# Top-2 gate and dispatch: the first group loaded in two parts and stored in four, without the small early store

## The chip, the cores and the metric

The kernel runs on one core of one Trainium2 chip. Its compute engines used here are DVE (VectorE) and ACT (ScalarE); SP (SyncE) and ACT issue the DMAs, which run on sixteen DMA engines. The metric is the device time of one execution in microseconds (us), and the time before is the median of three runs.

## The reference

For each of 16 x 1024 tokens there are a row of 512 float32 values and eight router logits. The two largest softmax probabilities are kept, in rising order, and divided by their sum; the row is written twice, once scaled by each.

```python
probs = np.exp(router_logits - logits_max)
probs = probs / np.sum(probs, axis=-1, keepdims=True)
topk_indices = np.argsort(probs, axis=-1)[..., -k:]
topk_probs = np.take_along_axis(probs, topk_indices, axis=-1)
topk_probs = topk_probs / np.sum(topk_probs, axis=-1, keepdims=True)
x_expanded = x[:, :, np.newaxis, :].repeat(k, axis=2)
return (x_expanded * topk_probs[..., np.newaxis]).astype(np.float32)
```

With k = 2 the two weights are sigmoids of the difference between the largest and the second largest logit, with either sign. The input x has 33.5 MB, the output 67.1 MB.

## The kernel before

A "row" in this text is one token on each of 128 partitions: 256 KB to load and 512 KB to store. The 16,384 tokens are 128 such rows, in two groups of 65 and 63 (GROUPS). In a group each partition holds consecutive tokens, so a load or a store of n rows is one contiguous stretch per partition.

Two buffers hold all the data. xs has room for 65 input rows. osp has room for 18 output rows (L), and its first rows also hold the logits and the scratch of the top-2 steps, until the weights WA are there. STORES gives for each store of a group the first row, the number of rows, where the output is built and at which place. Output that is built in "xs" overwrites input rows that have been used already, two places for each output row.

The group's loads are issued first, in the parts that LOADS gives (line 139), all on SP's queue but the first of the second group. After the load that completes the first six rows the two logit loads (lines 144 and 145) are issued, also on SP, and top2_weights computes the weights of both groups: eleven small DVE instructions (lines 26 to 36) and two sigmoids on ACT (lines 37 and 38).

Then each part of the group is multiplied on DVE (line 164) and stored (line 176). The first store of the first group, 3 rows, is issued by ACT; all the others by SP. SP and ACT work through their issues in program order, and an issue waits until the data are ready, with everything behind it on that queue.

A part that is built in osp from place 0 again is cut in two (cuts): the first FREE[g] rows lie where no store is under way, the others wait until the earlier store from the same places has landed. In the second group, ACT makes the last ACT_ROWS rows of the first part with one activation for each row and weight (line 157), and DVE the rest.

The second group's first load, 4 rows, is issued by ACT behind a small activation, the pause (line 128), which waits until the first group's last but one store has landed. The load of 28 rows follows the first group's last store on SP. The load of 31 rows goes into places from which the first group's last store reads, and waits for that store's landing.

Of the kernel before, what the change touches and what calls it, by code (L numbers as in the profile page):

```python
# [1 line left out]

# [4 lines left out]

F32 = mybir.dt.float32
ALU = mybir.AluOpType
ACTF = mybir.ActivationFunctionType  # L10
P = 128


def top2_weights(nc, WA, dlt, room, logits, E):

    tt = nc.vector.tensor_tensor
    hi, lo, n = None, None, E  # L20
    while n > 1:
        n //= 2
        if hi is None:
            a, b = logits[:, :, 0:n], logits[:, :, n : 2 * n]
            nhi, nlo = room(n), b
            tt(nhi, a, b, op=ALU.max)  # L26
            tt(nlo, a, b, op=ALU.min)  # L27
        else:
            a, b = hi[:, :, 0:n], hi[:, :, n : 2 * n]
            nhi, nlo, tmp = room(n), room(n), room(n)  # L30
            tt(tmp, lo[:, :, 0:n], lo[:, :, n : 2 * n], op=ALU.max)  # L31
            tt(nlo, a, b, op=ALU.min)  # L32
            tt(nlo, nlo, tmp, op=ALU.max)  # L33
            tt(nhi, a, b, op=ALU.max)  # L34
        hi, lo = nhi, nlo
    tt(dlt, hi[:, :, 0], lo[:, :, 0], op=ALU.subtract)  # L36
    nc.scalar.activation(WA[:, :, 0], dlt, ACTF.Sigmoid, scale=-1.0)  # L37
    nc.scalar.activation(WA[:, :, 1], dlt, ACTF.Sigmoid, scale=1.0)  # L38

GROUPS = [65, 63]

LOADS = [[6, 28, 31], [4, 28, 31]]
BASE = [0, 1]

STORES = [
    [(0, 3, "osp", 0), (3, 15, "osp", 3), (18, 16, "xs", 0), (34, 15, "osp", 0), (49, 16, "xs", 33)],
    [(0, 16, "osp", 2), (16, 16, "xs", 0), (32, 15, "osp", 0), (47, 16, "xs", 32)],
]  # L50

L = 18

FREE = [3, 2]

ACT_ROWS = 2


@with_exitstack
def kernel(  # L60
    ctx: ExitStack,
    tc: tile.TileContext,
    x: bass.AP,
    router_logits: bass.AP,
    k: bass.AP,
    out: bass.AP,
):
    nc = tc.nc
    B, S, D = x.shape
    E = router_logits.shape[-1]  # L70
    N = B * S
    assert int(k) == 2 and E == 8 and N == P * sum(GROUPS)
    M = N // P

    x_v, o_v, rl_v = [], [], []
    t0 = 0
    for n in GROUPS:
        t1 = t0 + P * n
        x_v.append(
            x.rearrange("b s d -> (b s) d")[t0:t1].rearrange("(p m) d -> p m d", p=P)  # L80
        )
        o_v.append(
            out.rearrange("b s k d -> (b s) k d")[t0:t1].rearrange(
                "(p m) k d -> p m k d", p=P
            )
        )
        rl_v.append(
            router_logits.rearrange("b s e -> (b s) e")[t0:t1].rearrange(
                "(p m) e -> p m e", p=P
            )  # L90
        )
        t0 = t1

    wpool = ctx.enter_context(tc.tile_pool(name="wpool", bufs=1))
    xs = wpool.tile([P, max(GROUPS), D], F32)
    osp = wpool.tile([P, L, 2, D], F32)
    WA = wpool.tile([P, M, 2], F32)
    dlt = wpool.tile([P, M], F32)


    flat = osp.rearrange("p l k d -> p (l k d)")
    taken = [0]

    def room(n):
        o = taken[0]
        taken[0] += M * n
        return flat[:, o : o + M * n].rearrange("p (m n) -> p m n", n=n)

    logits = room(E)

    def place(where, at, n):

        if where == "osp":
            return osp[:, at : at + n]
        return xs[:, at : at + 2 * n, :].rearrange("p (r k) d -> p r k d", k=2)

    m0 = 0
    stores = []
    for g, G in enumerate(GROUPS):
        x0, r = BASE[g], 0  # L120
        for n in LOADS[g]:

            late = g == 1 and r == 0
            if late:


                rows = xs[:, x0 : x0 + 2, :]
                pause = nc.scalar.activation(rows, rows, ACTF.Copy)  # L128
                tc.add_manual_dep(
                    pause.ins,  # L130
                    stores[-2].ins.name,
                    mybir.DependencyInfo(
                        mybir.DependencyClass.Sync, mybir.DependencyReason.DATA
                    ),
                    reason="begin when the store ahead of the last has landed",
                )
                tc.keep_in_program_order(pause)
            queue = nc.scalar if late else nc.sync
            load = queue.dma_start(xs[:, x0 + r : x0 + r + n, :], x_v[g][:, r : r + n, :])  # L139
            tc.keep_in_program_order(load)  # L140
            r += n
            if g == 0 and r == 6:
                n0 = GROUPS[0]
                tc.keep_in_program_order(nc.sync.dma_start(logits[:, :n0], rl_v[0]))  # L144
                tc.keep_in_program_order(nc.sync.dma_start(logits[:, n0:], rl_v[1]))  # L145
                top2_weights(nc, WA, dlt, room, logits, E)
        assert r == G
        for r, n, where, at in STORES[g]:
            og = place(where, at, n)

            again = where == "osp" and at == 0 and r > 0
            cuts = [0, FREE[g], n] if again else [0, n]
            if g == 1 and r == 0:
                cuts = [0, n - ACT_ROWS]
                for j in range(n - ACT_ROWS, n):
                    for k2 in range(2):
                        nc.scalar.activation(  # L157
                            og[:, j, k2, :],
                            xs[:, x0 + r + j, :],
                            ACTF.Copy,  # L160
                            scale=WA[:, m0 + r + j, k2 : k2 + 1],
                        )
            for a, b in zip(cuts, cuts[1:]):
                nc.vector.tensor_tensor(  # L164
                    og[:, a:b],
                    xs[:, x0 + r + a : x0 + r + b, :]
                    .unsqueeze(2)
                    .to_broadcast([P, b - a, 2, D]),
                    WA[:, m0 + r + a : m0 + r + b, :]
                    .unsqueeze(3)  # L170
                    .to_broadcast([P, b - a, 2, D]),
                    op=ALU.mult,
                )

            queue = nc.scalar if g == r == 0 else nc.sync
            stores.append(queue.dma_start(o_v[g][:, r : r + n], og))  # L176
            tc.keep_in_program_order(stores[-1])
        m0 += G


# [1 line left out]
_INS = ['x', 'router_logits', 'k']  # L182
_OUTS = [((16, 1024, 2, 512), 'float32')]

_NUMBERS = {'k': 2}


# [26 lines left out]
```

## Time and profile before

| | us |
|---|---|
| median of three runs (239.55 to 241.16) | 239.67 |
| the profiled execution | 239.64 |
| its span, first to last instruction | 237.9 |
| DVE busy | 139.8 |
| ACT busy | 5.4 |
| HBM read, written | 34.08 MB, 67.11 MB |

The span is what the profile covers of the execution; the remaining 1.7 us lie around it. The page divides the span into 40 slices of about 5.9 us. For each engine a digit gives the busy share of a slice in tenths; for DMA it is the mean busy share of the sixteen engines. Large packets are counted where they end, so neighbouring slices of the DMA line must be read together. A line of the timeline gives start, length, engine, line of code and operation; "SPq" and "ACTq" are issues of DMAs. A line of the DMA view gives what is moved, the issuing queue, the number of issues, their size where it is known and the median time from issue to landing. In a line of the groups the shape is partitions x elements; 1024 elements are one output row, and the last two numbers before the second bar are the busy time in us and the mean of one instruction in ns.

### The profile page before, as it was taken

Reading aid. Unit: us, or ns where it says so; the run is one execution under the profiler, and the core shown is the slowest. Engines: PE = TensorE matmul, PEld = TensorE weight load, DVE = VectorE, ACT = ScalarE, POOL = GpSimd, SP = SyncE. Lnnn points to the kernel's source line nnn. Section 1 sums busy time; section 2 is a strip of 40 time slices with the busy share of each in tenths; the row PEclk is TensorE's granted clock in tenths of the full one; section 3 lists DMA queues with packets and bytes.
Section 4 is the critical chain, followed back from the end, with each engine's and each line's share of the span. In section 5 each row is a group of like instructions: output and inputs, shape, how many; then the busy total and the mean of one; then the engine's idle time right before and its main releaser. Section 6 shows DMA issues by size and latency. Waiting matters only on the chain.

```text
span 237.9 us, 111 instructions
## 1 busy us (share of the span) xinstructions
DVE 139.8 (59%) x22; ACT 5.4 (2%) x8; POOL 0.2 (0%) x4
## 2 busy tenths in 40 slices
DVE  0650499999689999200000009999976999950000
ACT  2000000000000000010000003000000000000000
POOL 0000000000000000000000000000000000000000
DMA  7989998989998989989998999898998989989894
GB/s 266 550 357 481 441 408 375 486 351 496 397 463 353 529 362 465 496 353 415 555 397 350 444 479 470 384 507 364 485 397 386 496 353 507 465 362 518 353 529 176
DMA packets 2448, 101.19 MB, mean 425 GB/s; under 512 B 272, under 2 KB 400, under 8 KB 528
## 3 DMA queue, kind: packets, MB, share of 16 engines
q1 hardware_dynamic: 2160, 98.57, 96.2%
q10 hardware_dynamic: 288, 2.62, 2.6%
HBM read 34.08 MB, written 67.11 MB: 425 GB/s over the span
## 4 chain that ended last, share of the span: by engine, by line
DMA 49%; DVE 39%; SPq 1%; issue 0%; DVEq 0%
DMA xs<-in_x_dram 29%; DVE osp L164 25%; DMA out_dram<-osp 19%; DVE xs L164 14%; SPq L144 0%; SPq L145 0%; SPq L139 0%; SPq L176 0%; DVEq L164 0%
## 5 line engine op out<-in xcount | busy, mean ns | idle before, releaser
L164 DVE TENSOR_TENSOR osp<-xs,WA 128x3072 f32<-128x3072 f32 (+5 forms) x7 | 67.2, 9604 | 63.5 <-DMA xs<-in_x_dram 56.9
L164 DVE TENSOR_TENSOR xs<-xs,WA 128x16384 f32<-128x16384 f32 x4 | 68.9, 17225 | 0.2
L26 DVE TENSOR_TENSOR osp<-osp 128x512 f32<-128x512 f32 x1 | 0.7, 691 | 8.1 <-DMA osp<-in_router_logits_dram 8.1
L157 ACT ACTIVATE osp<-xs,WA 128x512 f32<-128x512 f32 x4 | 2.6, 709 | 37.6 <-DMA xs<-in_x_dram 37.6
L128 ACT ACTIVATE xs<-xs 128x1024 f32<-128x1024 f32 x1 | 1.1, 1056 | 91.1 <-DMA out_dram<-osp 91.1
L37 ACT ACT_TABLE_LOAD x1 | 1.3, 1283 | 0.7 <-PEq L195 0.7
L27 DVE TENSOR_TENSOR osp<-osp 128x512 f32<-128x512 f32 x1 | 0.7, 691 | 0.0
L32 DVE TENSOR_TENSOR osp<-osp 128x256 f32<-128x256 f32 (+1 forms) x2 | 0.7, 352 | 0.0
L34 DVE TENSOR_TENSOR osp<-osp 128x256 f32<-128x256 f32 (+1 forms) x2 | 0.7, 351 | 0.0
L33 DVE TENSOR_TENSOR osp<-osp 128x256 f32<-128x256 f32 (+1 forms) x2 | 0.7, 351 | 0.0
L31 DVE TENSOR_TENSOR osp<-osp 128x256 f32<-128x256 f32 (+1 forms) x2 | 0.7, 350 | 0.0
L37 ACT ACTIVATE WA<-dlt 128x128 f32<-128x128 f32 x1 | 0.3, 315 | 10.0 <-DVE dlt L36 10.0
L36 DVE TENSOR_TENSOR dlt<-osp 128x128 f32<-128x128 f32 x1 | 0.3, 291 | 0.0
L38 ACT ACTIVATE WA<-dlt 128x128 f32<-128x128 f32 x1 | 0.3, 298 | 0.0
L195 POOL MEMSET const-uint8-127<- 128x1 uint8 x1 | 0.1, 102 | 0.0
L195 POOL MEMSET const-bfloat16-1.0<- 128x1 bf16 x1 | 0.1, 101 | 0.0
L195 POOL MEMSET const-float32-0.0<- 128x1 f32 x1 | 0.1, 98 | 0.2 <-issue 0.2
L195 POOL MEMSET const-float32-1.0<- 128x1 f32 x1 | 0.1, 98 | 0.0
## 6 DMA issues: line engine op xcount, KB each, us to landing
out_dram<-osp SPq DMA_DIRECT2D x3, 7680.0 KB, 23.3
xs<-in_x_dram SPq DMA_DIRECT2D x2, 7936.0 KB, 40.7
xs<-in_x_dram SPq DMA_DIRECT2D x2, 7168.0 KB, 35.1
xs<-in_x_dram SPq DMA_DIRECT2D x1, 1536.0 KB, 5.9
out_dram<-osp ACTq DMA_DIRECT2D x1, 1536.0 KB, 24.8
xs<-in_x_dram ACTq DMA_DIRECT2D x1, 1024.0 KB, 24.8
osp<-in_router_logits_dram SPq DMA_DIRECT2D x1, 260.0 KB, 6.2
osp<-in_router_logits_dram SPq DMA_DIRECT2D x1, 252.0 KB, 6.3
```

The source lines that it names most:

```text
L26: tt(nhi, a, b, op=ALU.max)
L27: tt(nlo, a, b, op=ALU.min)
L31: tt(tmp, lo[:, :, 0:n], lo[:, :, n : 2 * n], op=ALU.max)
L32: tt(nlo, a, b, op=ALU.min)
L33: tt(nlo, nlo, tmp, op=ALU.max)
L34: tt(nhi, a, b, op=ALU.max)
L36: tt(dlt, hi[:, :, 0], lo[:, :, 0], op=ALU.subtract)
L37: nc.scalar.activation(WA[:, :, 0], dlt, ACTF.Sigmoid, scale=-1.0)
L128: pause = nc.scalar.activation(rows, rows, ACTF.Copy)
L157: nc.scalar.activation(og[:, j, k2, :], xs[:, x0 + r + j, :], ACTF.Copy, scale=WA[:, m0 + r + j, k2 : k2 + 1],)
L164: nc.vector.tensor_tensor(og[:, a:b], xs[:, x0 + r + a : x0 + r + b, :] .unsqueeze(2) .to_broadcast([P, b - a, 2, D]), WA[:, m0 + r + a : ...
L195: nc = _bacc.Bacc("TRN2", target_bir_lowering=False, num_devices=1)
```

## The change

The first group's loads become two, of 33 and 32 rows, and the logit loads and the top-2 steps follow the first of these. Its stores become four, of 16, 16, 17 and 16 rows. The first is built in osp from place 2 on, like that of the second group; ACT makes its last five rows in ten activations, DVE the other eleven, and SP issues the store, so that all stores are now on SP's queue. The part that uses osp again has two free rows instead of three, and fifteen that wait. The second group's tables are the same.

```diff
-LOADS = [[6, 28, 31], [4, 28, 31]]
+LOADS = [[33, 32], [4, 28, 31]]
...
-    [(0, 3, "osp", 0), (3, 15, "osp", 3), (18, 16, "xs", 0), (34, 15, "osp", 0), (49, 16, "xs", 33)],
+    [(0, 16, "osp", 2), (16, 16, "xs", 0), (32, 17, "osp", 0), (49, 16, "xs", 33)],
     [(0, 16, "osp", 2), (16, 16, "xs", 0), (32, 15, "osp", 0), (47, 16, "xs", 32)],
...
-FREE = [3, 2]
-
-ACT_ROWS = 2
+FREE = [2, 2]
+
+ACT_ROWS = [5, 2]
...
-            if g == 0 and r == 6:
+            if g == 0 and r == LOADS[0][0]:
...
-            if g == 1 and r == 0:
-                cuts = [0, n - ACT_ROWS]
-                for j in range(n - ACT_ROWS, n):
+            if r == 0:
+                cuts = [0, n - ACT_ROWS[g]]
+                for j in range(n - ACT_ROWS[g], n):
...
-            queue = nc.scalar if g == r == 0 else nc.sync
-            stores.append(queue.dma_start(o_v[g][:, r : r + n], og))
+            stores.append(nc.sync.dma_start(o_v[g][:, r : r + n], og))
```

## The prediction, made before the changed kernel ran

> **What bounds the kernel now.** I first read the page's totals, the slices of the span and the DMA queues.
>
> ```profile
> span 237.9 us, 111 instructions
> DVE 139.8 (59%) x22; ACT 5.4 (2%) x8; POOL 0.2 (0%) x4
> DMA  7989998989998989989998999898998989989894
> DMA packets 2448, 101.19 MB, mean 425 GB/s; under 512 B 272, under 2 KB 400, under 8 KB 528
> q1 hardware_dynamic: 2160, 98.57, 96.2%
> q10 hardware_dynamic: 288, 2.62, 2.6%
> DMA 49%; DVE 39%; SPq 1%; issue 0%; DVEq 0%
> ```
>
> The busiest compute engine works 59% of the span. The packets of the two DMA queues take 96.2 + 2.6 = 98.8% of the sixteen engines' span, and only the first and the last slice are thin. So the kernel is bound by DMA throughput without a hole: DVE matters only by when it lets a store be issued. The chain of waits, the last line, names DVE for 39%, but a store that is issued while older packets still run costs nothing; what counts is whether each queue entry is there before the packets ahead of it are gone.
>
> Next come the issues in the timeline (start, length, what), and for each the DMA view of its stretch, whose last figure is the time from issue to landing. First the opening, then the last store of the first group and the second group.
>
> ```profile
> 0.73 0.37 SPq L139 DMA_DIRECT2D xs<-in_x_dram  x1
> 2.10 1.05 SPq L139 DMA_DIRECT2D xs<-in_x_dram  x2
> 15.91 0.38 ACTq L176 DMA_DIRECT2D out_dram<-osp  x1
> 43.00 0.35 SPq L176 DMA_DIRECT2D out_dram<-osp  x1
> 79.13 0.33 SPq L176 DMA_DIRECT2D out_dram<-osp  x1
> 96.39 0.33 SPq L176 DMA_DIRECT2D out_dram<-xs  x1
> 124.71 0.34 SPq L139 DMA_DIRECT2D xs<-in_x_dram  x1
> 157.51 0.34 SPq L176 DMA_DIRECT2D out_dram<-osp  x1
> 211.64 0.33 SPq L176 DMA_DIRECT2D out_dram<-xs  x1
> ```
>
> ```profile
> xs<-in_x_dram SPq DMA_DIRECT2D x1, 1536.0 KB, 5.9
> xs<-in_x_dram SPq DMA_DIRECT2D x1, 7936.0 KB, 45.2
> out_dram<-osp ACTq DMA_DIRECT2D x1, 1536.0 KB, 24.8
> out_dram<-osp SPq DMA_DIRECT2D x1, 7680.0 KB, 23.1
> out_dram<-osp SPq DMA_DIRECT2D x1, 7680.0 KB, 24.4
> out_dram<-xs SPq DMA_DIRECT2D x1, 28.3
> xs<-in_x_dram SPq DMA_DIRECT2D x1, 7936.0 KB, 36.2
> out_dram<-osp SPq DMA_DIRECT2D x1, 22.8
> out_dram<-xs SPq DMA_DIRECT2D x1, 25.4
> ```
>
> Row by row the second fence belongs to the first; of the two loads issued at 2.10 it shows the second (31 rows), which starts at about 2.7. The landings are therefore 6.63, 47.9, 40.7, 66.1, 103.5, 124.7, 160.9, 180.3 and 237.0.
>
> The unit of the sum comes from the end, where nothing but stores runs: 47 rows are stored between the landings at 180.3 and 237.0, so one row of stores takes 56.7 / 47 = 1.207 us; a row of loads has half the bytes, 0.604. It holds elsewhere: the 15 rows after the last load took 66.1 - 47.9 = 18.2 us, 15 x 1.207 = 18.1. The start costs 5.9 - 6 x 0.604 = 2.28 us between the issue of a load on idle engines and its landing, beyond its data.
>
> **The change, part by part.** I rebuild the first group's clock.
>
> ```profile
> 8.05 0.69 DVE L26 TENSOR_TENSOR osp<-osp 128x512 f32<-128x512 f32 x1 [8.05 <-DMA osp<-in_router_logits_dram]
> 12.52 3.36 DVE L164 TENSOR_TENSOR osp<-xs,WA 128x3072 f32<-128x3072 f32 x1 [0.58 <-ACT WA L38]
> 142.25 2.56 ACT L157 ACTIVATE osp<-xs,WA 128x512 f32<-128x512 f32 x4 [37.57 <-DMA xs<-in_x_dram]
> 142.35 15.09 DVE L164 TENSOR_TENSOR osp<-xs,WA 128x14336 f32<-128x14336 f32 x1 [45.98 <-DMA xs<-in_x_dram]
> ```
>
> ```profile
> L164 DVE TENSOR_TENSOR xs<-xs,WA 128x16384 f32<-128x16384 f32 x4 | 68.9, 17225 | 0.2
> L164 DVE TENSOR_TENSOR osp<-xs,WA 128x15360 f32<-128x15360 f32 x1 | 16.2, 16157 | 10.9 <-DMA xs<-in_x_dram 10.9
> L164 DVE TENSOR_TENSOR osp<-xs,WA 128x13312 f32<-128x13312 f32 x1 | 14.0, 14026 | 3.4 <-DMA out_dram<-osp 3.4
> L164 DVE TENSOR_TENSOR osp<-xs,WA 128x12288 f32<-128x12288 f32 x1 | 13.0, 12960 | 2.6 <-DMA out_dram<-osp 2.6
> L164 DVE TENSOR_TENSOR osp<-xs,WA 128x2048 f32<-128x2048 f32 x1 | 2.3, 2285 | 0.0
> L157 ACT ACTIVATE osp<-xs,WA 128x512 f32<-128x512 f32 x4 | 2.6, 709 | 37.6 <-DMA xs<-in_x_dram 37.6
> ```
>
> *Loads in 33 and 32 rows.* The two logit loads stay behind the first load on SP's queue, which is now 27 rows longer: 27 x 0.604 = 16.3 us. So the chain of small DVE steps starts at 8.05 + 16.3 = 24.4 instead of 8.05, and the first multiply at 12.52 + 16.3 = 28.8. DVE idles through those 16.3 us; it is hidden as long as loads fill the engines. SP waits for nothing before the load of 32 rows, so that load follows at once.
>
> *First store.* DVE multiplies 11 rows. Between 12 and 13 rows the step is 14.026 - 12.960 = 1.066 us, so 11 rows take 11.89 and end at 40.7. ACT makes the other five rows in ten activations; four took 2.56 us, so ten take 6.4 and end at 35.2 if they run beside DVE. That they do is shown at 142: 14 rows took 15.09 beside four activations, while 12 and 15 rows without them (12.960, 16.157) give 15.09 by the same step. ACT's first activation waits for the load and the sigmoids; behind it on ACT stands only the pause for the second group, due near 103. The store is issued on SP at 40.74. Its wait holds up the second store on SP, which is not due before 57.9.
>
> *Early store removed.* Its 3 rows leave the stretch of the loads, 3 x 1.207 = 3.6 us of DMA time; the same bytes go out in later stores, so nothing is saved by that. The loads land at 47.9 - 3.6 = 44.3 with every other loss kept. The first store is then issued 44.3 - 40.74 = 3.5 us before they land. Is that enough? In the second group the store issued at 157.51 stood 160.9 - 157.5 = 3.4 us ahead of the last load's landing, and its 16 rows landed 180.3 - 160.9 = 19.4 us later, against 16 x 1.207 = 19.3. So a lead of 3.4 us lost no more than 0.1.
>
> *The reused rows of osp.* The first store lands at 44.3 + 19.3 = 63.6. Meanwhile DVE does 16 rows in place (17.225, to 57.9, second store issued) and the two free rows (2.285, to 60.2; the second of them needs the load that landed at 44.3). The other 15 rows wait for the landing at 63.6 and take 16.157: third store issued at 79.8. The second store lands at 63.6 + 19.3 = 82.9, so the lead is 3.1 us. No row shows exactly this lead. The nearest bounds are 2.28 us, all that a load on idle engines needed including its own start, and 3.4, shown to suffice for a store. I take it as enough, nearer to the 3.4 that concerns a store; at worst 0.3 us is lost.
>
> *After it.* The third store, one of 17 rows, lands at 82.9 + 17 x 1.207 = 103.4, before 103.5; the pause on ACT waits for just that landing. The fourth is issued at 79.8 + 17.2 = 97.0 instead of 96.4, while packets run until 103.4. SP then issues the load of 28 rows behind it, as before, and the last load waits for the fourth store to land, at 124.7 before. From there both kernels are the same, to the end.
>
> *What can be gained.* By units, the loads, the 512 KB of logits (two load rows) and the early store are 65 + 2 + 6 = 73 load rows, 44.1 us; with 0.73 of start and 2.28 of latency the last load would land at 47.1. It lands at 47.9, so 0.8 us is lost somewhere while the early store runs among the loads. If the mix causes all of it, all is gained; if reads alone or the first store on a queue causes it, nothing is. I take half, 0.4, as no row splits it. The pieces per partition stay eight for the first group: three loads and five stores before; after, two loads and four stores, of which the load of 33 rows is built as 2 x 8448 elements and the store of 17 as 2 x 8704.
>
> One rule speaks for a different result. By the rows, stores that follow each other land 19.3 us per 16 rows and 18.1 per 15, in proportion to bytes, so a transfer queued behind another shows no fixed price of its own. The Trainium skill, page DMA: Bandwidth & Descriptors, section Anatomy of one DMA, prices a transfer at about 2 us plus its bytes. Two transfers fewer would then save 4 us and give 235.6, an estimate by that page. Nothing here pays that price except at the start.
>
> **The rivals.** *A. The forecast:* no hole opens, 0 to 0.8 us gained.
>
> *B. A small hole ahead of the first or the third store.* The first is the case in which the change does not do what it says: the last load packets are gone before the store's first packet is there. For it: leads shrink from 47.9 - 43.0 = 4.9 us to 3.5, and to 3.1 at the third store. Against: the 3.4 shown to suffice. It decides when the lead falls under 2.3 to 3.4; each microsecond under costs one. A slip of one or two microseconds gives 239.7 to 241.0.
>
> *C. Slower: DVE and ACT hold each other up while both write the first store.* If ten activations of 709 ns were to run in series with the 11 rows, the issue would come at 40.74 + 7.1 = 47.8. With 2.28 us of lead needed, the hole would be 47.8 - (44.3 - 2.28) = 5.8 us, and the time 245.4. It costs from an issue at 42.0 on. Against it stands the 15.09 beside four activations; for it, only that ten at once are not in the trace.
>
> *D. Faster: a fixed price per transfer.* Fifteen transfers instead of seventeen; if each costs its 2.28 us of latency, 4.6 us go, and the time is 235.0. The landings in proportion to rows speak against it. This is the mechanism of the page's rule above.
>
> **How the numbers follow.** The profiled execution took 239.64 us, 1.74 more than its span of 237.9; the median of three runs is 239.67, with a range up to 241.16, so the profiled one is an ordinary run. A gives 239.64 - 0.4 = 239.2, and 238.8 to 239.7 as its own range. Chances: A 0.76, B 0.14, C 0.07, D 0.03. A difference of about 1%, 2.4 us, is what a measurement here can tell from no change. Only D is faster than that: 0.03. Slower by that much are most of C and a large B: 0.08. The rest, 0.89, is the same. For 8 in 10 the range takes A and the smaller half of B, with 0.2 for scatter below: 238.6 to 240.5.
>
> **What would show it.** In the changed profile: DVE's first small step near 24.4, first multiply near 28.8 and 11.9 us long, the first store issued near 40.7 while its landing comes 16 x 1.207 us after that of the 32-row load, at 43.5 to 44.3. The third store issued near 79.8 and landing near 103.4 or up to 0.8 earlier; DMA share still near 98.8%. A thin slice near 43 or 82 would mean B or C; C would show as a multiply longer than 12 us. A span shorter by more than 0.8 us would prove the unit of the sum wrong.

## The result, and the profile after

The changed kernel takes 240.96 us, the median of 15 runs (240.18 to 241.94), against 239.64 for the kernel before in the same comparison (239.49 to 241.16): a ratio of 1.0051, with a 95% interval of 1.0034 to 1.0067. It is slower by about half a per cent, where 239.2 was forecast. Its runs also spread far more: 13 of the 15 runs of the kernel before lie between 239.49 and 239.70, while those of the changed kernel fill 1.8 us evenly. The profiled execution took 240.59.

The page after, first its totals, the slices of DVE and DMA and the queues:

```profile
span 238.8 us, 118 instructions
DVE 134.3 (56%) x21; ACT 11.5 (5%) x18; POOL 0.2 (0%) x4
...
DVE  0000799999599999200000019999966999950000
...
DMA  7999999898989899999999979798989897998984
...
DMA packets 2416, 101.19 MB, mean 424 GB/s; under 512 B 240, under 2 KB 368, under 8 KB 496
...
q1 hardware_dynamic: 2272, 100.14, 97.3%
q10 hardware_dynamic: 144, 1.05, 1.0%
```

No slice of the DMA line is thin between the first and the last: each 7 stands beside a 9, and a packet is counted as a whole in the slice where it begins (not where it ends, as is said ahead of the prediction). The timeline of the changed kernel, as far as it answers to the rows shown before:

```profile
24.82 0.69 DVE L26 TENSOR_TENSOR osp<-osp 128x512 f32<-128x512 f32 x1 [24.82 <-DMA osp<-in_router_logits_dram]
...
29.16 6.22 ACT L157 ACTIVATE osp<-xs,WA 128x512 f32<-128x512 f32 x10
29.29 11.89 DVE L164 TENSOR_TENSOR osp<-xs,WA 128x11264 f32<-128x11264 f32 x1 [0.58 <-ACT WA L38]
41.28 0.35 SPq L175 DMA_DIRECT2D out_dram<-osp  x1
...
58.54 0.34 SPq L175 DMA_DIRECT2D out_dram<-xs  x1
63.48 16.16 DVE L164 TENSOR_TENSOR osp<-xs,WA 128x15360 f32<-128x15360 f32 x1 [2.76 <-DMA out_dram<-osp]
79.66 0.38 SPq L175 DMA_DIRECT2D out_dram<-osp  x1
...
124.77 0.34 SPq L139 DMA_DIRECT2D xs<-in_x_dram  x1
...
157.69 0.34 SPq L175 DMA_DIRECT2D out_dram<-osp  x1
...
181.23 14.03 DVE L164 TENSOR_TENSOR osp<-xs,WA 128x13312 f32<-128x13312 f32 x1 [4.10 <-DMA out_dram<-osp]
...
212.55 0.33 SPq L175 DMA_DIRECT2D out_dram<-xs  x1
```

And the DMA view of the changed kernel, from issue to landing in the last column: the load of 32 rows issued at 2.18, the stores issued at 41.28, 58.54 and 79.66, the load issued at 124.77, and the stores issued at 157.69 and 212.55.

```profile
xs<-in_x_dram SPq DMA_DIRECT2D x1, 41.9
...
out_dram<-osp SPq DMA_DIRECT2D x1, 22.2
...
out_dram<-xs SPq DMA_DIRECT2D x1, 24.2
...
out_dram<-osp SPq DMA_DIRECT2D x1, 8704.0 KB, 23.6
...
xs<-in_x_dram SPq DMA_DIRECT2D x1, 7936.0 KB, 37.0
...
out_dram<-osp SPq DMA_DIRECT2D x1, 23.5
...
out_dram<-xs SPq DMA_DIRECT2D x1, 25.4
```

The landings are 44.1, 63.5, 82.7, 103.3, 161.8, 181.2 and 237.95. At 103.3 the changed kernel is 0.3 us ahead of its forerunner (103.5). At 124.77 it is 0.06 behind (124.71), so about 0.3 was lost there, and between 124.8 and 161.8 it loses 0.8 more: the last load takes 37.0 us to land instead of 36.2. That difference then stays to the end (237.95 against 237.0). So nothing is lost in the loads and stores that were changed; 0.3 is lost at the end of the first group's fourth store and 0.8 in the second group, and the code of both is the same as before.

The packet records tell how. They do not name the engine, but each packet begins where another ends, so they fall into sixteen unbroken rows with nearly the same bytes (6.3 MB each); each row is taken here as one DMA engine. In the kernel before all sixteen end between 236.2 and 236.7 us. In the changed one fifteen end between 236.0 and 236.4, earlier than before, and one at 237.6. On that engine a single packet took 0.81 us longer than its fifteen fellows' of the same size: its last load packet of the second group, begun at 158.36, after the first store of that group had been issued at 157.69. The last store lands at 237.95, 0.4 us after this engine's end and 1.6 after the last of the fifteen others, so one late engine sets the time of the kernel.

That engine was late already. It began this packet 0.42 us after the next latest engine, for it had lost 0.56 us, the most of the sixteen, on a packet of the first group's fourth store begun at 121.11. A packet begun after the issue is not always stretched: in the kernel before all sixteen last load packets began 0.24 to 0.73 us after the issue at 157.51, and none was.

### The profile page after: what moved, and what is told of

Read it like the earlier page. It is cut to its first block, busy times and chain, and to the rows that moved or that the text cites. A ratio compares the mean times of both kernels' runs of the same rounds, so it can differ in the third digit from the quotient of the medians.

```text
span 238.8 us, 118 instructions
## 1 busy us (share of the span) xinstructions
DVE 134.3 (56%) x21; ACT 11.5 (5%) x18; POOL 0.2 (0%) x4
## 4 chain that ended last, share of the span: by engine, by line
DMA 48%; DVE 40%; SPq 1%; issue 0%; ACT 0%; DVEq 0%
DVE osp L164 24%; DMA out_dram<-osp 19%; DMA xs<-in_x_dram 19%; DVE xs L164 14%; DMA osp<-in_router_logits_dram 10%; DVE osp L26 0%; DVE osp L27 0%; DVE osp L33 0%; DVE osp L31 0%; DVE osp L34 0%; DVE osp L32 0%; SPq L144 0%; SPq L139 0%; SPq L175 0%; ACT WA L38 0%
## 5 line engine op out<-in xcount | busy, mean ns | idle before, releaser
L164 DVE TENSOR_TENSOR osp<-xs,WA 128x2048 f32<-128x2048 f32 (+4 forms) x6 | 61.7, 10290 | 53.1 <-DMA xs<-in_x_dram 45.6
L157 ACT ACTIVATE osp<-xs,WA 128x512 f32<-128x512 f32 x14 | 8.8, 707 | 38.0 <-DMA xs<-in_x_dram 38.0
```

Of the source, the lines that this page charges most:

```text
L157: nc.scalar.activation(og[:, j, k2, :], xs[:, x0 + r + j, :], ACTF.Copy, scale=WA[:, m0 + r + j, k2 : k2 + 1],)
L164: nc.vector.tensor_tensor(og[:, a:b], xs[:, x0 + r + a : x0 + r + b, :] .unsqueeze(2) .to_broadcast([P, b - a, 2, D]), WA[:, m0 + r + a : ...
```

## The experiments

The theory to test, called the race below: when a store is already queued as an engine begins its last load packets, one of these packets is stretched by up to a microsecond or more; when the store comes after the last of them has begun, it isn't. The stretch is unequal among engines and differs between runs. Rivals: the removed early store had kept such turns cheap; the large first load puts the engines out of step; the leads of the stores are too short after all.

**The changed kernel again**, for a second trace.

> The changed kernel as it is, on another chip session, for a second trace. Its first trace had no hole in the DMA stream, but one of the sixteen engines ended about 1.2 us after the other fifteen, which all ended earlier than before. If lateness of single engines is what costs the time, this run again shows no hole, fifteen engines near 237.4 us and one or more behind, at a place that may differ, and 240.2 to 242. If the leads of the first and third store are the cause (a hole in some runs), a gap appears between the packets near 43 or 82 us, of 0.5 to 2 us on all engines.

240.95 us (240.13 to 242.29 in 11 runs). Again there is no hole. The profiled run, one of 240.26, has four engines with stretched last load packets near 158 (0.04, 0.09, 0.43 and 0.60 us; the two that lost most had begun last). Fourteen engines end between 236.05 and 236.45, the other two at 236.9 and 237.27. The fifteen of the first trace had ended by 236.4, not near 237.4 as the expectation has it. The lateness is that of single engines.

**First store on ACT's queue:**

```diff
-            stores.append(nc.sync.dma_start(o_v[g][:, r : r + n], og))
+            queue = nc.scalar if g == r == 0 else nc.sync
+            stores.append(queue.dma_start(o_v[g][:, r : r + n], og))
```

> The changed kernel, but its first store (16 rows) is issued by ACT as before. If it is the single queue that costs (no second queue in the first 100 us), this gives 239.4 to 239.8. If the missing early store or the large first load costs, it stays at 240.6 to 241.3. If a hole ahead of the first store costs, it stays too, since the issue comes at the same time.

242.16 us (242.11 to 242.65), ratio 1.0106 (1.0088 to 1.0123): worse than either. On a queue of its own the first store shares the engines with the second store, lands later, and the 15 rows that wait for its place follow; the third store is issued at 82.71, when the engines have nothing left, and all stand still together for 0.7 us (0.9 per engine on average). Besides, the first packet of the first store is stretched on every engine, by 0.84 us on average. The run speaks against the queue as the only cause, as 242.16 less the hole of 0.9 is still above 241; it also brought a loss of its own, so it does not settle what the queue does. The changed kernel has no such hole.

**The kernel before with its early store on SP's queue**, behind the loads:

```diff
-            queue = nc.scalar if g == r == 0 else nc.sync
+            queue = nc.sync
```

> The kernel before, with only the queue of its 3-row store changed from ACT to SP, so that the store runs behind the loads of the first group and no longer among them. If stores among the loads keep the time down (the mix, or the second queue), this loses what the change lost: 240.6 to 241.3. If the large first load or the leads are the cause, it stays at 239.4 to 239.8, as its loads and leads are those of before or longer.

240.21 us (240.04 to 240.33 in 12 runs), ratio 1.0013 (1.0000 to 1.0027). Half a microsecond is lost with the loads and sizes of before, so moving the early store out of the loads does cost, though less than the whole. The windows show where. The columns are: the stretch of time, its length, the busy time of DVE, ACT and POOL with the number of instructions, the TensorE clock, the DMA share and the GB/s. The last two count a packet as a whole where it begins, so equal GB/s with a larger share means longer packets. First the kernel before, then this one:

```profile
22.00:24.00 2.00, 0.00 (x0) 0.00 (x0) 0.00 (x0) 1.00 1.49 557
...
40.00:42.00 2.00, 2.00 (x1) 0.00 (x0) 0.00 (x0) 1.00 1.18 508
...
44.00:46.00 2.00, 2.00 (x1) 0.00 (x0) 0.00 (x0) 1.00 1.25 508
```

```profile
40.00:42.00 2.00, 1.97 (x2) 0.00 (x0) 0.00 (x0) 1.00 1.68 508
```

At 508 GB/s the ordinary share is 1.18. Here the last load packets, begun between 40 and 42, have 1.68: (1.68 - 1.18) x 2 us = 1.0 us per engine on average (0.74 to 1.23 in the packet records). In the kernel before the last load packets, begun between 44 and 46, have 1.25, only 0.14 us too much. But there the load packets that follow the early store's start had been stretched already: at 22, 557 GB/s should take 557 / 508 x 1.18 = 1.29, and it is 1.49, so 0.4 us.

**A small first load in the changed kernel:**

```diff
-LOADS = [[33, 32], [4, 28, 31]]
+LOADS = [[6, 27, 32], [4, 28, 31]]
```

> The changed kernel, but its first load is 6 rows again (6, 27, 32 rows), with the logits behind them, so that the weights are ready early and the first store is issued about 5 us sooner (near 36 us). If the large first load puts the engines out of step, or if the lead of the first store is short, this returns to 239.2 to 239.7. If the missing early store costs, it stays at 240.6 to 241.3.

241.67 us (240.09 to 242.54), ratio 1.0074 (1.0046 to 1.0101). A small first load and a longer lead don't help; the first store, issued near 36.5, now comes well ahead of the last load packets, and these are stretched. Its window, and below it that of the changed kernel with the same bytes:

```profile
40.00:42.00 2.00, 2.00 (x1) 0.00 (x0) 0.00 (x0) 1.00 1.75 524
```

```profile
40.00:42.00 2.00, 1.90 (x2) 0.00 (x0) 0.00 (x0) 1.00 1.21 524
```

That is (1.75 - 1.21) x 2 = 1.1 us per engine. The changed kernel, whose first store is issued at 41.28, has none of it. Near 121, however, this version has next to none of the stretch that the changed kernel has there (a later experiment returns to it), for 1.22 is its ordinary share at 524 GB/s:

```profile
120.00:122.00 2.00, 0.00 (x0) 0.00 (x0) 0.00 (x0) 1.00 1.22 524
```

The profiled run, of 240.09, is the fastest of the six, so what the slower ones lose beyond this 1.1 us is not shown.

**The second group's first store later:**

```diff
-ACT_ROWS = [5, 2]
+ACT_ROWS = [5, 1]
```

> The changed kernel, with ACT making one row instead of two of the second group's first store, so that this store is issued about 1.07 us later (near 158.7, while the last load packets, started at 157.6 to 158.4, run until about 160). Theory of the race: an engine loses 0.5 to 1.2 us when the descriptors of a store reach it before it has begun its last load packet, and nothing when they come after; in the changed kernel some engines are hit at the second group's turn and others not, which sets the slowest engine back and makes the runs spread from 240.1 to 242.3. Then nobody is hit here: no packet near 158 is stretched, and the time is 239.2 to 239.9 with a spread under 0.4 us. Rival, the large first load puts the engines out of step: no change, 240.1 to 242.3, median about 240.9. Rival, shortage of lead: 1 us later makes a hole near 160 and the time rises to about 241.5 or more.

240.18 us (239.55 to 240.95 in 12 runs), ratio 1.0017 (0.9998 to 1.0035). Issued at 158.94, the store stretches no packet near 158, and the fastest runs reach those of the kernel before. The median falls by 0.8 us, but it stays 0.5 above the kernel before and the spread doesn't shrink as the race alone says: something else stays.

**The second group's first store earlier:**

```diff
-ACT_ROWS = [5, 2]
+ACT_ROWS = [5, 5]
```

> The changed kernel, with ACT making five rows of the second group's first store, so that it is issued about 3.2 us earlier (near 154.5), ahead of every engine's last load packet. Race: all engines are hit alike, each by about 1 us, near 157 to 160: 240.4 to 241.0 with a small spread. First load out of step: no change in median or spread. Shortage of lead: faster, 239.2 to 239.7.

242.08 us (241.01 to 242.58), ratio 1.0099 (1.0081 to 1.0116). Now all sixteen engines are hit, by 0.15 to 1.31 us. The window of this kernel, and below it that of the changed kernel with the same GB/s:

```profile
156.00:158.00 2.00, 2.00 (x1) 0.00 (x0) 0.00 (x0) 1.00 1.43 508
```

```profile
156.00:158.00 2.00, 1.91 (x2) 0.00 (x0) 0.00 (x0) 1.00 1.17 508
```

The rise is larger than expected. In the profiled run, of 241.15, the hits are unequal (0.61 on average), and the engine hit worst ends last.

**The first group's first store earlier:**

```diff
-ACT_ROWS = [5, 2]
+ACT_ROWS = [7, 2]
```

> The changed kernel, with ACT making seven rows of the first group's first store, so that it is issued about 2.1 us earlier (near 39.1), ahead of every engine's last load packet of that group. Race: every engine's last load packet is now stretched by about 1 us near 41 (it was not in the changed kernel), so the fastest runs rise from 240.2 to about 241, with the second group's spread on top. Shortage of lead: faster than the changed kernel, 239.2 to 239.7. First load out of step: no change.

242.57 us (242.18 to 243.05 in 4 runs), ratio 1.0122 (1.0109 to 1.0135). Two microseconds more of lead, issue at 39.06, cost 1.6 us. Its window has a share of 1.67, against 1.21 in the changed kernel, so 0.9 us per engine. Two engines lose another microsecond near 160: a microsecond behind the others, they are the only ones that begin their last load packet after the store's issue, at 159.38.

```profile
40.00:42.00 2.00, 2.00 (x1) 0.00 (x0) 0.00 (x0) 1.00 1.67 524
```

**The kernel before with the second group's first store later:**

```diff
-ACT_ROWS = 2
+ACT_ROWS = 1
```

> The kernel before, with ACT making one row instead of two of the second group's first store (issue near 158.6). In the kernel before no engine was hit in the profiled run, but 3 of 15 runs were 0.6 to 1.5 us longer than the rest. Race: those stragglers go and the median stays at 239.6. Shortage of lead: a hole near 160 and 240 or more. First load out of step: nothing changes, stragglers included.

239.65 us (239.57 to 240.16 in 11 runs), ratio 1.0001 (0.9993 to 1.0010). As expected of the race: the median stays and no straggler is above 240.2, where the kernel before had one of 23 at 241.67. So few stragglers prove little.

**All late, with a small first load:**

```diff
-LOADS = [[33, 32], [4, 28, 31]]
+LOADS = [[6, 27, 32], [4, 28, 31]]
...
-ACT_ROWS = [5, 2]
+ACT_ROWS = [0, 1]
```

> Loads of 6, 27 and 32 rows with the logits behind the first, no early store, and DVE alone makes the 16 rows of the first store (ACT none), so that it is issued near 41.8 us, after each engine's last load packet of the first group has begun; the second group's store is issued near 158.8 (ACT one row). Race: no stretched packet at 40 nor at 158, and the start of the kernel before: 238.9 to 239.4, a little faster than before, with a small spread. First load out of step: also 239.0 to 239.6, since the first load is small. If the missing early store itself costs (by whatever means), it stays above 240. Shortage of lead: a hole near 43 and 240.5 or more.

240.75 us (240.27 to 242.16), ratio 1.0054 (1.0033 to 1.0075): the race alone and the large first load are contradicted, the missing early store (above 240) is not. Of a hole near 43 there are only traces, up to 0.13 us on a few engines. The last load packets of the first group are clean, as planned. Instead, the packets of the first group's last store are stretched near 107 (0.3 us on average) and near 121 (0.5), and one engine falls behind there. The load of 28 rows lands with that engine, so the second group's store was issued at 160.00 and not 158.8.

**The logits ahead of the large first load**, with the same late stores:

```diff
-ACT_ROWS = [5, 2]
+ACT_ROWS = [0, 1]
...
+    n0 = GROUPS[0]
+    tc.keep_in_program_order(nc.sync.dma_start(logits[:, :n0], rl_v[0]))
+    tc.keep_in_program_order(nc.sync.dma_start(logits[:, n0:], rl_v[1]))
     m0 = 0
...
             if g == 0 and r == LOADS[0][0]:
-                n0 = GROUPS[0]
-                tc.keep_in_program_order(nc.sync.dma_start(logits[:, :n0], rl_v[0]))
-                tc.keep_in_program_order(nc.sync.dma_start(logits[:, n0:], rl_v[1]))
                 top2_weights(nc, WA, dlt, room, logits, E)
```

> Loads of 33 and 32 rows with the logits ahead of both on the queue, DVE alone makes the first store's 16 rows (issue near 41.4), ACT one row of the second group's. It has the late first and second stores of the kernel above, but the large first load. Race alone: 239.0 to 239.6 like the kernel above. If the large first load also costs (engines out of step from the start), it keeps the spread of the late-store version, 239.6 to 241, median near 240.2.

242.67 us (241.14 to 244.28), ratio 1.0123 (1.0087 to 1.0159). The first store came later than meant, at 43.08; the engines stood still before 44, for 0.7 us on average, and the stretches near 108 and 122 are as above. It doesn't separate the theories.

**The second group's first store later still:**

```diff
-ACT_ROWS = [5, 2]
+ACT_ROWS = [5, 0]
```

> The changed kernel, with ACT making no row of the second group's first store, which is issued another 1.07 us later (near 159.9), with about 1 us left until the last load lands. It measures the lead that a store needs. If under 1 us is enough, no hole, and the time is as with one row, median 240.2. If about 2 us are needed, the stream has a hole of 0.5 to 1 us on all engines near 160.5, and the median is 240.6 to 241.2.

240.72 us (240.25 to 240.99 in 5 runs). The store is issued at 159.92, when the first engines run dry; the first store packet begins at 160.76. So here a store needed 0.84 us from issue to its first packet. Counted to the landing of the loads, a lead of 1.3 us was too short (161.2 - 159.9), and 2.3 was enough: with the issue at 158.94 above and the landing at 161.3, no engine had a hole.

**The small first load with the second group's store later:**

```diff
-LOADS = [[33, 32], [4, 28, 31]]
+LOADS = [[6, 27, 32], [4, 28, 31]]
...
-ACT_ROWS = [5, 2]
+ACT_ROWS = [5, 1]
```

> The version with loads of 6, 27 and 32 rows and a first store issued early (near 36.5 us), with ACT making one row instead of two of the second group's first store (issue near 159.0). Race at the second group's turn: its spread (240.1 to 242.5) goes, leaving the stall of about 1 us that all engines share near 40: 239.9 to 240.4, median 240.1. If the missing early store does its harm elsewhere than at that turn, the median stays near 241.5.

241.20 us (240.84 to 241.83), ratio 1.0061 (1.0044 to 1.0078). The spread shrinks from 2.5 to 1.0 us, but the median stays a microsecond above 240.1. In the profiled run one engine lost 0.6 us near 122, and the store, issued at 160.42, left holes near 161. The second group's turn is thus not where most of this version's loss arises.

**The early store put back, with a small first load:**

```diff
-LOADS = [[33, 32], [4, 28, 31]]
+LOADS = [[6, 27, 32], [4, 28, 31]]
...
-    [(0, 16, "osp", 2), (16, 16, "xs", 0), (32, 17, "osp", 0), (49, 16, "xs", 33)],
+    [(0, 3, "osp", 0), (3, 13, "osp", 3), (16, 16, "xs", 0), (32, 17, "osp", 0), (49, 16, "xs", 33)],
...
-FREE = [2, 2]
+FREE = [3, 2]
...
-ACT_ROWS = [5, 2]
+ACT_ROWS = [0, 2]
...
-            stores.append(nc.sync.dma_start(o_v[g][:, r : r + n], og))
+            queue = nc.scalar if g == r == 0 else nc.sync
+            stores.append(queue.dma_start(o_v[g][:, r : r + n], og))
```

> The version with loads of 6, 27 and 32 rows, with the early store put back: 3 rows issued by ACT near 16 us, among the loads, then stores of 13, 16, 17 and 16 rows. The store of 13 rows is issued near 40 us, well ahead of the last load packets. If the early store among the loads is what keeps the turns to stores cheap, this returns to 239.5 to 239.9 from 241.7, with stretched packets near 18, 23 and 45 of 0.7 us an engine in all, and none near 121. If the load sizes or the 17-row store cost, or the turn costs whatever came before, it stays at 240.3 or above.

239.91 us (239.51 to 242.41 in 12 runs), ratio 1.0018 (0.9995 to 1.0042), against 241.67 without the early store; half of the runs are at 239.51 to 239.83, the others reach up to 242.41. The stretches of the profiled run, the fastest, are those of the kernel before, at 22 and hardly any at 44, and none at 120, although the store of 13 rows is issued at 40.23, long before the last load packets:

```profile
22.00:24.00 2.00, 0.00 (x0) 0.00 (x0) 0.00 (x0) 1.00 1.45 541
44.00:46.00 2.00, 2.00 (x1) 0.00 (x0) 0.00 (x0) 1.00 1.24 524
120.00:122.00 2.00, 0.00 (x0) 0.00 (x0) 0.00 (x0) 1.00 1.36 590
```

The changed kernel at that last place, with the same GB/s:

```profile
120.00:122.00 2.00, 0.00 (x0) 0.00 (x0) 0.00 (x0) 1.00 1.48 590
```

There the changed kernel loses (1.48 - 1.36) x 2 = 0.24 us on average. With the same load sizes the early store, on its own queue, thus brings the median down by 1.8 us and makes the first turn to stores cheap. The second queue and the 13 rows of the next store come with it; no run varies them alone. The stretch near 121 is another matter. The version with 6, 27 and 32 rows and the early store on SP's queue have no store among the loads either, and hardly any of it. In the packet records it goes with the load of 33 rows: 0.21 to 0.26 us on average in the six traces that have this load and no hole in the first group, and 0.08 or less in the seven with a first load of 6 rows and no such hole, with the early store or without.

**The early store with the loads of 33 and 32 rows:** the stores, FREE, ACT_ROWS and queue of the kernel above, but the loads of the changed one.

> The changed kernel with its loads of 33 and 32 rows, and an early store of 3 rows issued by ACT as soon as the weights are there (near 32 us, among the load of 32 rows), then 13, 16, 17 and 16 rows. The store of 13 rows is issued near 46 us, when the last load packets run. If the early store is what matters, 239.4 to 240.0. If the load of 33 rows is what matters, it stays at 240.4 to 241.2 with its spread. Shortage of lead: a hole near 47 and 240.5.

242.65 us (242.22 to 242.76), ratio 1.0116 (1.0101 to 1.0132). It can't answer: the store of 13 rows was over before DVE had finished the next 16, whose store was issued at 63.74, and all engines stood still for 0.7 us near 64.

**The early store put back and the second group's store later:** the version of 239.91 with

```diff
-ACT_ROWS = [0, 2]
+ACT_ROWS = [0, 1]
```

> The version with loads of 6, 27 and 32 rows and the early store put back, with ACT making one row instead of two of the second group's first store (issue near 158.4 instead of 157.4). That version had a median of 239.91, with 7 of 12 runs at 239.5 to 239.85 and stragglers up to 242.4. Race at the second group's turn: the stragglers go, median 239.5 to 239.7, the best of all versions though hardly below the kernel before. If the stragglers come from elsewhere (the load sizes, the start), they stay and the median too.

239.86 us (239.73 to 240.61 in 11 runs), ratio 0.9998 (0.9977 to 1.0018). The longest run falls from 242.4 to 240.6, the fastest rise by 0.2; it is not to be told from the kernel before. No version was faster than the kernel before.

From the packet records of the profiled runs, this is how much longer than usual for their size the packets were, as a mean over the sixteen engines in us (the start is that of the first load; two dashes stand for under 0.03):

```
                        start  loads/early  last loads   near   near   ends of the
                               store 17-24    40-45      121    158    16 engines
before                  0.48      0.57         0.16       --     --    236.2-236.7
changed                 0.76       --           --       0.23   0.05   236.0-237.6
changed, again          0.72       --           --       0.21   0.07   236.1-237.3
second group later      0.62       --           --       0.22    --    236.1-237.0
second group earlier    0.75       --           --       0.24   0.61   236.5-238.2
first group earlier     0.60       --          0.93      0.24   0.13   236.8-239.5
early store on SP       0.59       --          1.03       --     --    236.5-237.2
6, 27, 32 rows          0.50       --          1.07       --     --    236.6-237.1
same, early store back  0.53      0.47         0.06       --     --    236.2-236.5
```

## Why the prediction was wrong

*What bounds the kernel, and the unit of the sum.* Right. DMA stays the bound, and the stores behind each other land 19.3 us per 16 rows (82.7 - 63.5 = 19.2).

*The first group's clock.* Right within 0.6 us: first small step at 24.82 (24.4 forecast), first multiply at 29.29 and 11.89 long (28.8, 11.89), ten activations beside it in 6.22 (6.4), first store issued at 41.28 (40.74), third at 79.66 (79.8) and landed at 103.3 (103.4). The lead of the first store is 44.1 - 41.28 = 2.8 us instead of 3.5, since the loads landed 0.2 earlier and the store was issued 0.5 later, and it sufficed. The need was overestimated: 2.3 us of lead were enough and 1.3 too few, with 0.84 us from issue to first packet.

*Rivals B, C and D.* No hole, so B did not happen; that the time fell in the place that was priced for B is chance. DVE and ACT did not hinder each other, so not C. D expected a fixed price per transfer, and two transfers fewer saved none of it; the landings in proportion to rows had said so, and the rule of the page of the Trainium skill on DMA, read as a price of each queued transfer, disagrees with them. That section is on DMAs that GpSimd issues; SP and ACT issue these.

*What can be gained.* The sum for the loss of the early store's stretch was right in size (0.8 forecast, 0.57 + 0.16 measured), and it did go: fifteen engines end earlier than before. But 0.28 came back at the start, which had been costed at the old start's price, and 0.23 near 121. The 0.28 is that of one pair of traces: over all traces the start costs about 0.5 to 0.6 with a first load of 6 rows and 0.6 to 0.8 with one of 33.

*The step that failed* is the assumption of the first part, that a store that is issued while older packets still run costs nothing, and its consequence, "From there both kernels are the same, to the end." The time at which a store is queued does have a price on the loads ahead of it. In the first group the change happened to hit the cheap moment. The second group has the same code in both kernels and, within 0.2 us, the same issue of its first store, but its engines come to that turn differently: after the change one or two of them, the last to begin, lose 0.4 to 0.8 us on their last load packet, and the last one sets the end. Moving that one store shows that its time has a price: 242.08 when 3.1 us earlier, 240.95 as it is, 240.18 when 1.3 us later. The latter is still 0.5 above the kernel before, so this turn is the larger part of the loss and not all of it. That the removed early store matters is shown by putting it back, 241.67 to 239.91, in a version with a small first load; moving it behind the loads in the kernel before costs 0.5. How much of the changed kernel's own loss is due to it is not shown, as the run with its load sizes and the early store had a hole elsewhere. That the mix could be worth keeping was not among the rivals: removing it was priced from zero to a gain, with no bound on the other side.

What stays open: why an early store among the loads makes the first turn to stores cheap, which the runs show but don't explain; why the load of 33 rows goes with stretched packets near 121, and why the four versions in which engines stood still in the first group have about 0.5 us there and 0.3 near 108; and what the runs near 242 us look like, since the profiled runs of the changed kernel and of the version with 6, 27 and 32 rows were among their faster ones. The Trainium skill, page DMA: Bandwidth & Descriptors, section Two DMAs through the same engine are not ordered, says that an engine's read and write sides are separate queues and that the descriptors within one queue are pipelined. A store whose reading begins while the last load is still being written would fit the stretch; no run here shows the two sides apart.

## What to carry to other kernels

When the DMA engines are full, look at how long packets take and which engine ends last, not only for holes: windows with equal GB/s and unequal shares show it. Queueing a store early is not free where the direction turns from loads to stores; here, without a small store among the loads, the cheap moment lay between one and two microseconds before the loads ran out, while about four cost 0.9 us, and about five 0.6 on average and 1.3 on the worst engine. A small store that runs among the loads may look like a nuisance and still pay for itself, so try its removal alone before building a schedule on it.

## What the runs showed of the hardware that was not expected

A store queued behind loads stretched the last load packets of the first group by 0.9 to 1.1 us on average when it was issued 1.5 us or more before they began (1.03, 1.07 and 0.93 in the table), but by 0.16 and 0.06 where a small store had run among the loads. In the second group, issued 3 us before, it was 0.61. The stretch is unequal: there it ran from 0.15 to 1.31 us among the sixteen engines at one turn, and in this trace, as in both of the changed kernel, the engine that began last lost most. Packets of a store are stretched too where loads are queued behind it: near 121 by 0.2 us on average with a first load of 33 rows. So are the first packets of the kernel, by 0.5 to 0.6 us on average with a first load of 6 rows and by 0.6 to 0.8 with one of 33.
